# The pooling mixer multiplies by its weights first and takes the running means as a band of coefficients on TensorE

## The chip, the cores and the metric

The kernel runs on one core of a Trainium2 chip. A run's time is the device time of one execution in microseconds (us); the time of a kernel is the median of its runs. One execution is also profiled, and all rows below come from that one.

## What is computed

Two layers of a decoder on 512 tokens of 1024 channels. Each layer is a feed-forward network (FFN), a token mixer and a second FFN, each behind a norm with a learned shift and scale. The mixer of layer 0 is the pooling mixer, cut here to what matters:

```python
POOL_WINDOWS = (2, 4, 8, 16)      # one for each group of 256 channels
for gi, w in enumerate(POOL_WINDOWS):
    ...
    outs.append((cs[..., sl] - prev) / cnt - hf[..., sl])   # trailing mean of w tokens minus the token
pooled = jnp.stack(outs, axis=2)
mixed = jnp.einsum('bsgc,gcd->bsgd', pooled, w_grp.astype(jnp.float32))
return (mixed.reshape(b_, s_, d_) * scale.astype(jnp.float32)).astype(h.dtype)
```

The mean runs over tokens and the weights over channels, so the two can be taken in either order.

## The kernel before

Activations lie with channels on the 128 partitions: `x` is 128 x 8 x 512 (partition, channel tile `kt` or `dt`, token). The tokens are worked in two halves of 256 wherever a norm follows, so that one half is normed on the other engines while TensorE works on the other half.

An FFN ends in `closing`: for each half, eight output tiles `dt` of 18 matmuls each (three matmuls of 256 columns, `mm3`, for each of six weight tiles), so 144 matmuls a half. VectorE adds each result into `x` (`update`, L225), ScalarE squares it (L174), GpSimd adds the squares (L175). After a half, `pool_then` is called: `rsig` sums the squares over partitions with two one-column matmuls (L197), VectorE and GpSimd make the reciprocal root (L199, L201), VectorE lays it on a diagonal (L203), and one matmul spreads it over the partitions (L207).

Then `Pooling.means` norms the eight tiles of the half (VectorE `t` L387, ScalarE `h` L389), adds shifted copies until the window is full (L396, on GpSimd for the widest window, on VectorE for the others), repairs the first tokens (L401) and makes mean minus token (L412, tiles `made`). `mix` multiplies by the weights: two matmuls of 256 columns for each output tile (L422), `update`, and the sum of squares for the next norm on TensorE (`sumsq_pe`, L181, one matmul for each tile). `pool_then` for half 0 makes means only; for half 1 it mixes half 0, makes the means of half 1, norms half 0 for the next FFN (`norm`, L216 to L219), mixes half 1 and norms it. The next FFN begins with the same two halves, three weight tiles of 48 matmuls each (`up`).

Result tiles of TensorE come from a pool of five PSUM banks (`bank()`, tag `mm`), handed out in the order in which the program asks. Weights arrive by DMA as `raw`; ScalarE and VectorE split them into `wh` and `wl` (L151, L152). A scheduler puts the instructions of each engine into one fixed order when the kernel is built; an engine then takes them in that order.

Of the kernel before, what the change touches and what calls it, by code (L numbers as in the profile page):

```python
# [7 lines left out]
F32 = mybir.dt.float32  # L8
F32R = mybir.dt.float32r
AF = mybir.ActivationFunctionType  # L10
ALU = mybir.AluOpType
# [4 lines left out]
P = 128  # L16
D = 1024
KT = D // P
S = 512
# [9 lines left out]
GH = HEADS // NG  # L29
GC = GH * HD  # L30
WINDOWS = (2, 4, 8, 16)
EPS = 1e-6
BIG = 1e30
LAG = 3
# [2 lines left out]
HALVES = ((0, S // 2), (S // 2, S // 2))  # L37
# [3 lines left out]
def trunk(  # L41
    ctx: ExitStack,
    tc: tile.TileContext,
    x_in, x_rows, c_in, ada_w, ada_b, norm_g, w_in, w_out, w_end, pool_w, pool_scale,
    fox_qkv, fox_f, fox_bf, fox_gain, fox_o, consts, edges, out,
):
    nc = tc.nc
    pe, act, dve, gp = nc.tensor, nc.scalar, nc.vector, nc.gpsimd
# [7 lines left out]
    tmp = ctx.enter_context(tc.tile_pool(name="tmp", bufs=2))  # L56
# [8 lines left out]
    def bank(tag="mm"):  # L65
        return banks[tag].tile([P, S], F32, tag=tag, name=tag)
# [12 lines left out]
    ng = pers.tile([P, DEPTH * 3, KT], F32, name="ng")  # L79
    ab = pers.tile([P, DEPTH * 3, 3 * KT], F32, name="ab")  # L80
    x = pers.tile([P, KT, S], F32, name="x")
# [101 lines left out]
    def rsig(acc, t0, tn, summed=False):  # L183
# [10 lines left out]
        else:  # L194
            st = bank("s")
            for b in range(bn):
                pe.matmul(st[:, b:b + 1], acc[:, (b0 + b) * P:(b0 + b + 1) * P], ones[:, 0:1],  # L197
                          start=True, stop=True)
        dve.tensor_scalar(out=v[:, :bn], in0=st[:, :bn], scalar1=1.0 / D, scalar2=EPS,  # L199
                          op0=ALU.mult, op1=ALU.add)  # L200
# [21 lines left out]
    def update(y, i, dt, t0, tn, acc, gate=None, sums=sumsq):  # L222
        sl = slice(t0, t0 + tn)
        g = (mods[i]["g"] if gate is None else gate)[:, dt:dt + 1]
        dve.scalar_tensor_tensor(out=x[:, dt, sl], in0=y, scalar=g, in1=x[:, dt, sl],  # L225
                                 op0=ALU.mult, op1=ALU.add)
        if acc is not None:
            sums(acc, dt, t0, tn)
        else:
            nc.sync.dma_start(out[:, dt, sl], x[:, dt, sl])  # L230
# [5 lines left out]
    class Feed:  # L236


        def __init__(self, w):
            self.units = [(w_in[w, j], [P, 2, KT, P], 2) for j in range(JC)]  # L240
            for ci in range(2):
                self.units += [(w_out[w, ci, dt], [P, JC, P], 4) for dt in range(KT)]
                j0, nj = CHUNKS[ci + 1]
                self.units += [(w_in[w, j], [P, 2, KT, P], 2) for j in range(j0, j0 + nj)]
            self.units += [(w_end[w, u], [P, 16, P], 4) for u in range(KT * (NJ - 2 * JC) // 16)]
            self.made = []
            self.depth = len(slots["pools"])
# [113 lines left out]


    class Pooling:
        def __init__(self, i, pool, w):
            self.i, self.pool, self.w = i, pool, w
            self.scale = pool.tile([P, KT], F32, name="sc")
            nc.sync.dma_start(self.scale, pool_scale)
            dve.tensor_tensor(out=self.scale, in0=self.scale, in1=mods[i]["g"], op=ALU.mult)
            self.edges = pool.tile([P, 4, 16], F32, name="ed")
            nc.sync.dma_start(self.edges, edges)  # L370
            self.tails = pool.tile([P, KT, 16], F32, name="tails")
            gp.memset(self.tails, 0.0)

        def means(self, r, t0, tn):

            m = mods[self.i]
            sl = slice(t0, t0 + tn)
            hs, wins, made = {}, {}, {}
            for gi in (3, 0, 1, 2):
                eng, w = gp if gi == 3 else dve, WINDOWS[gi]  # L380
                two = slice(2 * gi, 2 * gi + 2)
                h = hs[gi] = self.pool.tile([P, 2, 16 + tn], F32, tag="h", name="h", bufs=3)
                eng.tensor_copy(h[:, :, :16], self.tails[:, two])
                for k in range(2):
                    kt = 2 * gi + k
                    t1 = tmp.tile([P, tn], F32, tag="t1", name="t1")
                    dve.scalar_tensor_tensor(out=t1, in0=x[:, kt, sl], scalar=m["a"][:, kt:kt + 1],  # L387
                                             in1=r[:, :tn], op0=ALU.mult, op1=ALU.mult)
                    act.activation(h[:, k, 16:], t1, AF.Identity, bias=m["s"][:, kt:kt + 1])  # L389
                if t0 == 0:  # L390
                    act.activation(self.tails[:, two], h[:, :, tn:], AF.Copy)
                cur, step = h, 1
                while step < w:
                    nxt = self.pool.tile([P, 2, 16 + tn], F32, tag=f"win{gi // 3}", name="win", bufs=2)
                    a = 16 - (w - 2 * step)
                    eng.tensor_tensor(out=nxt[:, :, a:], in0=cur[:, :, a:],  # L396
                                      in1=cur[:, :, a - step:16 + tn - step], op=ALU.add)
                    cur, step = nxt, 2 * step
                win = wins[gi] = cur[:, :, 16:]
                if t0 == 0:  # L400
                    eng.tensor_tensor(  # L401
                        out=win[:, :, :w - 1], in0=win[:, :, :w - 1],
                        in1=self.edges[:, gi, :w - 1].unsqueeze(1).to_broadcast([P, 2, w - 1]),
                        op=ALU.mult)
                if gi < 3:
                    made[gi] = self.pooled(gi, win, hs[gi])
            made[3] = self.pooled(3, wins[3], hs[3])
            return made

        def pooled(self, gi, win, h):  # L410
            made = self.pool.tile([P, 2, S // 2], F32, tag="made", name="made", bufs=4)
            dve.scalar_tensor_tensor(out=made, in0=win, scalar=1.0 / WINDOWS[gi], in1=h[:, :, 16:],  # L412
                                     op0=ALU.mult, op1=ALU.subtract)
            return made

        def mix(self, made, t0, tn):

            sums = bank()
            for dt in range(KT):
                y = bank()  # L420
                for ct in range(2):
                    pe.matmul(y[:, :tn], self.w[:, 2 * dt + ct], made[dt // 2][:, ct], start=ct == 0,  # L422
                              stop=ct == 1)
                update(y[:, :tn], self.i, dt, t0, tn, sums, gate=self.scale, sums=sumsq_pe)
            return sums

# [22 lines left out]
    def fox(i, early_pool, first, second_half, then):  # L449
        acc2 = new_acc()  # L450
        with tc.tile_pool(name="fox", bufs=1, reuse_waits="tile") as fp:
# [46 lines left out]
            def projections(grp):  # L498
# [18 lines left out]
                def block(role, b):  # L517
# [6 lines left out]
                    if role == 2:  # L524
# [8 lines left out]
                                      op=ALU.add)  # L533
                    dve.tensor_scalar(out=v, in0=v, scalar1=1.0 / HD, scalar2=EPS, op0=ALU.mult,
                                      op1=ALU.add)
# [181 lines left out]
    with tc.tile_pool(name="more", bufs=1, side="right", reuse_waits="tile") as more:  # L717
# [3 lines left out]
        with tc.tile_pool(name="start", bufs=2, reuse_waits="tile") as sp, in_order, ExitStack() as early:  # L721
# [15 lines left out]
            act.activation(cond, cond, AF.Silu)  # L737
            dve.tensor_scalar(out=v, in0=v, scalar1=1.0 / D, scalar2=EPS, op0=ALU.mult, op1=ALU.add)
            gp.tensor_tensor(out=v, in0=v, in1=mhalf[:, :NTB], op=ALU.pow)
# [33 lines left out]
            for kt in range(KT):  # L773
                t1 = sp.tile([P, S], F32, tag="t1", name="t1")
                act.activation(t1, x[:, kt], AF.Identity, scale=mods[0]["a"][:, kt:kt + 1],
                               bias=mods[0]["s"][:, kt:kt + 1])
# [23 lines left out]
        ahead = []  # L800
# [10 lines left out]
        with tc.tile_pool(name="poolw", bufs=1, side="right", reuse_waits="tile") as pw:  # L811
            pw_all = pw.tile([P, 16, P], F32, name="poolw")
            pooling = []
            opened = ExitStack()

            def pool_then(acc, t0, tn):
                r = rsig(acc, t0, tn)
                if t0 == 0:
                    pool = opened.enter_context(tc.tile_pool(name="pool", bufs=1, reuse_waits="tile"))
                    pooling.append(Pooling(1, pool, pw_all))  # L820
                    pooling.append(pooling[0].means(r, t0, tn))
                    return
                sums = pooling[0].mix(pooling[1], *HALVES[0])
                made = pooling[0].means(r, t0, tn)
                norm(2, sums, *HALVES[0], True)
                sums = pooling[0].mix(made, t0, tn)
                ahead.append(Feed(1))
                ahead[0].fetch(len(slots["pools"]))
                norm(2, sums, t0, tn, True)
                opened.close()  # L830

            jobs = ada_jobs(0, False) + ada_jobs(1)
            jobs += [(lambda pool: nc.sync.dma_start(pw_all, pool_w), lambda _: None)] + ada_jobs(2)
            feed = Feed(0)
            feed.units = feed.units[4:]
            ffn(0, feed, jobs, pool_then, begin, started=4)
# [80 lines left out]
```

## Time and profile before

| | |
|---|---|
| median of 3 runs | 1829.47 us (1829.47, 1829.47, 1833.93) |
| the profiled execution | 1832.36 us |
| its span | 1830.6 us |
| TensorE busy | 98% of the span |
| VectorE, ScalarE, GpSimd busy | 54%, 34%, 6% |

The span is what the profile shows; 1.8 us lie around it. TensorE is nearly always busy, so what matters is where it is not. Busy ends of matmuls are modelled; how fast they follow each other is read from their starts.

### The profile page before, as it was taken

Reading aid. Unit: us, or ns where it says so; the run is one execution under the profiler, and the core shown is the slowest. Engines: PE = TensorE matmul, PEld = TensorE weight load, DVE = VectorE, ACT = ScalarE, POOL = GpSimd, SP = SyncE. Lnnn points to the kernel's source line nnn. Section 1 sums busy time; section 2 is a strip of 40 time slices with the busy share of each in tenths; the row PEclk is TensorE's granted clock in tenths of the full one; section 3 lists DMA queues with packets and bytes.
Section 4 is the critical chain, followed back from the end, with each engine's and each line's share of the span. In section 5 each row is a group of like instructions: output and inputs, shape, how many; then the busy total and the mean of one; then the engine's idle time right before and its main releaser. Section 6 shows DMA issues by size and latency. Waiting matters only on the chain.

```text
span 1830.6 us, 24017 instructions
## 1 busy us (share of the span) xinstructions
PE 1794.5 (98%) x9564; PEld 1543.5 (84%) x9564; DVE 989.8 (54%) x1963; ACT 624.8 (34%) x1258; POOL 107.6 (6%) x118
## 2 busy tenths in 40 slices
PE   6999999989999999999999999999999999999999
PEld 5888888879888888998888889989997888888887
DVE  7567466386466473363453634577677553432433
ACT  6323223244223232242232333455454342222231
POOL 0000000050000000110000001221110200000000
PEclk9999999999999999999999999999999899999999
DMA  9457466211366452231543431122212021321421
GB/s 367 188 204 269 181 231 229 93 70 64 121 252 245 174 218 99 70 138 70 202 159 144 174 131 69 48 76 72 80 59 87 12 105 58 126 99 63 138 92 69
DMA packets 45857, 244.73 MB, mean 134 GB/s; under 512 B 5409, under 2 KB 10017, under 8 KB 21937
## 3 DMA queue, kind: packets, MB, share of 16 engines
q1 hardware_dynamic: 45744, 243.20, 36.3%
q8 instruction: 75, 1.23, 0.3%
q14 instruction: 38, 0.30, 0.1%
HBM read 241.05 MB, written 2.13 MB: 133 GB/s over the span
## 4 chain that ended last, share of the span: by engine, by line
PE 95%; DVE 4%; ACT 1%; issue 0%; DMA 0%; POOL 0%; SPq 0%; ACTq 0%; DVEq 0%; POOLq 0%
PE mm L164 28%; PE mm L165 27%; PE mm L163 27%; PE s L163 3%; PE s L165 3%; PE s L164 3%; PE mm L592 2%; DVE wl L152 1%; PE mm L618 1%; PE mm L595 1%; DVE x L225 0%; DVE win L396 0%; DMA rows<-x_rows 0%; DVE t L387 0%; PE mm L422 0%
## 5 line engine op out<-in xcount | busy, mean ns | idle before, releaser
L164 PE MATMUL mm<-hlo,wh 128*128 128x512 f32 (+1 forms) x1512 | 560.4, 372 | 2.8 <-DVE hlo L786 2.8
L165 PE MATMUL mm<-hhi,wl 128*128 128x512 f32 (+1 forms) x1512 | 558.0, 371 | 0.5 <-DVE wl L152 0.5
L163 PE MATMUL mm<-hhi,wh 128*128 128x512 f32 (+1 forms) x1512 | 554.5, 372 | 1.6 <-ACT hhi L777 1.3
L151 ACT ACTIVATE wh<-raw 128x256 fp32r<-128x256 f32 (+2 forms) x528 | 311.6, 654 | 576.6 <-PE mm L164 322.7
L152 DVE TENSOR_TENSOR wl<-raw,wh 128x256 fp32r<-128x256 f32 (+2 forms) x528 | 359.8, 734 | 59.0 <-ACT wh L151 54.8
L164 PEld LDWEIGHTS mm<-hlo,wh 128*128 128x128 f32 x1512 | 284.5, 188 | 52.3 <-DVE hlo L786 3.3
L163 PEld LDWEIGHTS mm<-hhi,wh 128*128 128x128 f32 x1512 | 283.2, 189 | 52.2 <-ACT hhi L777 1.7
L165 PEld LDWEIGHTS mm<-hhi,wl 128*128 128x128 f32 x1512 | 284.4, 188 | 49.9 <-DVE wl L152 0.7
L290 DVE TENSOR_TENSOR sil<-sil,mm 128x512 f32<-128x512 f32 (+1 forms) x95 | 61.0, 642 | 460.1 <-PE mm L165 443.0
L164 PE MATMUL mm<-gl,wh 128*128 128x512 f32 (+1 forms) x848 | 299.0, 353 | 0.0
L165 PE MATMUL mm<-gh,wl 128*128 128x512 f32 (+1 forms) x848 | 298.3, 353 | 0.0
L163 PE MATMUL mm<-gh,wh 128*128 128x512 f32 (+1 forms) x848 | 297.7, 354 | 0.0
L165 PEld LDWEIGHTS mm<-gh,wl 128*128 128x128 f32 x848 | 160.3, 189 | 21.9
L164 PEld LDWEIGHTS mm<-gl,wh 128*128 128x128 f32 x848 | 160.3, 189 | 21.9
L163 PEld LDWEIGHTS mm<-gh,wh 128*128 128x128 f32 x848 | 159.7, 189 | 22.0
L100 DVE CUSTOM_DVE_ANT_0 ada<-ada,cond 128x1024 f32<-128x1024 f32 x144 | 170.2, 1219 | 0.7 <-DMA ada<-ada_w 0.6
L289 ACT ACTIVATE sil<-mm 128x512 f32<-128x512 f32 (+1 forms) x94 | 52.5, 559 | 237.6 <-PE mm L165 236.4
L337 DVE SCALAR_TENSOR_TENSOR x<-mm,mg,x 128x512 f32<-128x512 f32 x64 | 48.0, 749 | 99.2 <-PE mm L165 98.3
L175 POOL TENSOR_TENSOR acc<-acc,sq 128x256 f32<-128x256 f32 x56 | 49.8, 889 | 866.3 <-ACT sq L174 535.2
L163 PE MATMUL s<-wh,hhi 128*128 128x256 f32 x288 | 84.2, 292 | 3.5 <-DVE qk L551 3.5
L165 PE MATMUL s<-wh,hlo 128*128 128x256 f32 x288 | 82.8, 288 | 0.0
L164 PE MATMUL s<-wl,hhi 128*128 128x256 f32 x288 | 82.6, 287 | 0.0
(173 smaller groups left out, 1656.6 us busy)
## 6 DMA issues: line engine op xcount, KB each, us to landing
raw<-w_in SPq DMA_DIRECT2D x84, 1024.0 KB, 5.1
ada<-ada_w SPq DMA_DIRECT2D x72, 1024.0 KB, 5.0
raw<-w_out SPq DMA_DIRECT2D x64, 512.0 KB, 5.6
raw<-w_end SPq DMA_DIRECT2D x12, 1024.0 KB, 4.8
raw<-fox_qkv SPq DMA_DIRECT2D x12, 1024.0 KB, 4.8
raw<-w_in SPq DMA_DIRECT2D x16, 256.0 KB, 8.0
cb<-cum SPq DMA_DIRECT2D x16, 256.0 KB, 3.4
raw<-fox_o SPq DMA_DIRECT2D x4, 1024.0 KB, 4.8
```

The source lines that it names most:

```text
L100: dve.tensor_tensor_reduce(out=raw[:, r, :], in0=raw[:, r, :], in1=cond, scale=1.0, scalar=0.0, op0=ALU.mult, op1=ALU.add, accum_out=mods[ ...
L151: act.activation(hi[:, c:c + n], src[:, c:c + n], AF.Copy)
L152: dve.tensor_tensor(out=lo[:, c:c + n], in0=src[:, c:c + n], in1=hi[:, c:c + n].bitcast(F32), op=ALU.subtract)
L163: pe.matmul(o, lh, rh, start=start, stop=False)
L164: pe.matmul(o, lh, rl, start=False, stop=False)
L165: pe.matmul(o, ll, rh, start=False, stop=stop)
L175: gp.tensor_tensor(out=acc[:, sl], in0=acc[:, sl], in1=sq, op=ALU.add)
L289: act.activation(sil[:, :tn], gu[0][:, :tn], AF.Silu)
L290: dve.tensor_tensor(out=sil[:, :tn], in0=sil[:, :tn], in1=gu[1][:, :tn], op=ALU.mult)
L337: done = dve.scalar_tensor_tensor(out=x[:, dt, :], in0=y, scalar=mods[i]["g"][:, dt:dt + 1], in1=x[:, dt, :], op0=ALU.mult, op1=ALU.add)
L592: pe.matmul(s[hh][:, :n], self.q[m == 2][rows, self.pair, b * P:n], self.k[m == 1][rows, self.pair, :n], start=m == 0, stop=False)
L595: pe.matmul(s[hh][:, b * P:n], mr[:, 0, :], mr[:, 1, :], start=False, stop=True)
```

## The change

The order of the two linear steps is turned round. `spread` makes the normed `h` as before, without windows. `product` multiplies: `h` is now the stationary operand (128 channels by 128 tokens) and the weights are the moving one, so that the result `z` has tokens on partitions; a half is two blocks of 128 tokens, 16 matmuls of 256 columns, and ScalarE copies four banks of 512 columns out to `z`. `mix` takes the means with a constant matrix `bands` of 128 x 143 for each window (mean minus token): for each output tile and block one matmul of 128 columns (`own`, L412) and, for every block but the first, one of 15 columns for the tokens that look back into the block before (`carry`, L416). All window work on VectorE and GpSimd, the tails and the edge repair are gone.

```diff
-        def means(self, r, t0, tn):
...
+        def spread(self, r, t0, tn):
...
+            h = self.pool.tile([P, KT, tn], F32, tag="h", name="h", bufs=2)
+            for kt in range(KT):
+                t1 = tmp.tile([P, tn], F32, tag="t1", name="t1")
+                dve.scalar_tensor_tensor(out=t1, in0=x[:, kt, t0:t0 + tn], scalar=m["a"][:, kt:kt + 1],
+                                         in1=r[:, :tn], op0=ALU.mult, op1=ALU.mult)
+                act.activation(h[:, kt], t1, AF.Identity, bias=m["s"][:, kt:kt + 1])
+            return h
+
+        def product(self, h, t0, tn):
+
+            ng = len(WINDOWS) // 2
+            for b in range(tn // P):
+                z = self.z[t0 // P + b] = self.pool.tile([P, D], F32, tag="z", name="z", bufs=3)
+                for c in range(2):
+                    o = bank()
+                    for g in range(ng):
+                        og = o[:, g * 2 * P:(g + 1) * 2 * P].rearrange("p (d q) -> p d q", q=P)
+                        for ct in range(2):
+                            gi = c * ng + g
+                            pe.matmul(og, h[:, 2 * gi + ct, b * P:(b + 1) * P], self.w[:, gi, ct],
+                                      start=ct == 0, stop=ct == 1)
+                    act.activation(z[:, c * S:(c + 1) * S], o, AF.Copy)
+
+        def mix(self, t0, tn):
 
             sums = bank()
             for dt in range(KT):
                 y = bank()
-                for ct in range(2):
-                    pe.matmul(y[:, :tn], self.w[:, 2 * dt + ct], made[dt // 2][:, ct], start=ct == 0,
-                              stop=ct == 1)
+                cols = slice(dt * P, (dt + 1) * P)
+                for b in range(tn // P):
+                    n = t0 // P + b
+                    own = self.bands[:, int(n == 0), dt // 2]
+                    pe.matmul(y[:, b * P:(b + 1) * P], self.z[n][:, cols], own[:, :P], start=True,
+                              stop=n == 0)
+                    if n:
+                        last = self.bands[:, int(n == 1), dt // 2]
+                        pe.matmul(y[:, b * P:b * P + REACH], self.z[n - 1][:, cols], last[:, P:],
+                                  start=False, stop=True)
                 update(y[:, :tn], self.i, dt, t0, tn, sums, gate=self.scale, sums=sumsq_pe)
             return sums
...
-                    pooling.append(pooling[0].means(r, t0, tn))
+                    pooling[0].product(pooling[0].spread(r, t0, tn), t0, tn)
                     return
-                sums = pooling[0].mix(pooling[1], *HALVES[0])
-                made = pooling[0].means(r, t0, tn)
+                sums = pooling[0].mix(*HALVES[0])
+                h = pooling[0].spread(r, t0, tn)
                 norm(2, sums, *HALVES[0], True)
-                sums = pooling[0].mix(made, t0, tn)
+                pooling[0].product(h, t0, tn)
+                sums = pooling[0].mix(t0, tn)
```

Line numbers shift by one in the changed kernel (L163 to L165 are L164 to L166, L197 is L198, L207 is L208), and the product stands in L399. The matmuls of the pooling mixer change as follows.

| | before | after |
|---|---|---|
| weights, 256 columns | 32 | 32 |
| `own`, 128 columns | 0 | 32 |
| `carry`, 15 columns | 0 | 24 |

**The first place, on TensorE's queue.** This is where half 0 of the closing of the first FFN has ended and its norm begins. Before, 37 matmuls of half 1 already stand ahead of the two one-column matmuls, and 32 and then 75 more follow with the spreading matmul between them:

```order
L165 MATMUL mm<-gh,wl 128x256
L163 MATMUL mm<-gh,wh 128x256
L197 MATMUL s<-ones,acc 128x1 x2
L164 MATMUL mm<-gl,wh 128x256
L165 MATMUL mm<-gh,wl 128x256
L163 MATMUL mm<-gh,wh 128x256
```

Now the 144th matmul of half 0 is the last one ahead of them:

```order
L164 MATMUL mm<-gh,wh 128x256
L165 MATMUL mm<-gl,wh 128x256
L166 MATMUL mm<-gh,wl 128x256
L198 MATMUL s<-ones,acc 128x1 x2
L208 MATMUL s<-dg,ones 128x256
L399 MATMUL mm<-poolw,h 128x256 x10
L164 MATMUL mm<-gh,wh 128x256
L165 MATMUL mm<-gl,wh 128x256
L166 MATMUL mm<-gh,wl 128x256
L164 MATMUL mm<-gh,wh 128x256
L399 MATMUL mm<-poolw,h 128x256 x6
```

What moved: the norm of half 0 and the whole product of half 0 (16 matmuls) now stand ahead of 140 of the 144 matmuls of half 1.

**The second place, on TensorE's queue.** This is the end of half 1 of the closing. Before, the weights follow (`made` by `poolw`), with a sum of squares (L181) among them:

```order
L165 MATMUL mm<-gh,wl 128x256
L422 MATMUL mm<-made,poolw 128x256 x2
L181 MATMUL mm<-sq,ones 128x256
L422 MATMUL mm<-made,poolw 128x256 x2
L197 MATMUL s<-ones,acc 128x1 x2
L422 MATMUL mm<-made,poolw 128x256 x4
```

Now:

```order
L166 MATMUL mm<-gh,wl 128x256
L412 MATMUL mm<-bands,z 128x128 x2
L416 MATMUL mm<-bands,z 128x15
L182 MATMUL mm<-sq,ones 128x256
L412 MATMUL mm<-bands,z 128x128 x2
L416 MATMUL mm<-bands,z 128x15
```

What moved: the sum of squares of the first output tile now stands behind three short matmuls.

**The third place, on ScalarE's queue**, at the same point of the program: the splitting of the third weight tile of the next FFN (`wh<-raw`) and the squares of the last closing tile (L175) and of the first mixed tiles (L181):

```order
L175 ACTIVATE sq<-x 128x256 x2
L152 ACTIVATE wh<-raw 128x1024
L175 ACTIVATE sq<-x 128x256
L152 ACTIVATE wh<-raw 128x1024
L175 ACTIVATE sq<-x 128x256 x2
L152 ACTIVATE wh<-raw 128x1024 x2
L175 ACTIVATE sq<-x 128x256
L181 ACTIVATE sq<-x 128x256 x5
```

Before, it stood like this:

```order
L389 ACTIVATE h<-t_2759,ms_919 128x256
L389 ACTIVATE h<-t_2762,ms_919 128x256
L174 ACTIVATE sq<-x 128x256
L391 ACTIVATE tails<-h 128x32
L151 ACTIVATE wh<-raw 128x1024 x2
L389 ACTIVATE h<-t_2775,ms_919 128x256
L174 ACTIVATE sq<-x 128x256
```

What moved: behind the third pair of splittings there stood an `h` and a square of half 1; now the last square of half 1 and all squares of the mix stand there.

## Rows read from the trace of the kernel before

**Rows 1.** Stretches of 10 us: PE, PEld, DVE, ACT, POOL busy; PEclk, DMA share, GB/s

```profile
380.00:390.00 10.00, 7.85 (x63) 7.39 (x61) 9.98 (x14) 7.54 (x16) 9.55 (x8) 1.00 0.30 105
390.00:400.00 10.00, 6.80 (x19) 5.53 (x20) 9.57 (x19) 2.01 (x6) 3.53 (x4) 0.66 0.56 206
400.00:410.00 10.00, 8.41 (x37) 6.43 (x35) 10.00 (x23) 6.01 (x14) 5.15 (x4) 1.00 0.00 0
```

**Rows 2.** Chain that ended last, from 360 to 440 us: start, us, what

```profile
373.30 0.34 PE s L197 x4
...
376.21 2.35 DVE wl L152 x2
...
381.33 0.98 DVE win L396
...
414.76 3.45 PE mm L422 x16
...
420.71 0.47 PE mm L163 x4
```

**Rows 3.** Tile `win` alone in one stretch: DVE busy, POOL busy, PEclk, DMA share, GB/s

```profile
374.00:426.00 52.00, 16.83 (x23) 10.80 (x9) 0.93 0.18 61
```

**Rows 4.** Timeline where half 0 ends: start, us, instruction, [idle before <-what ended it]

```profile
368.58 0.28 PE L165 MATMUL mm<-gh,wl 128*128 128x256 f32 x1
...
368.90 0.48 DVE L225 SCALAR_TENSOR_TENSOR x<-mm,mg,x 128x256 f32<-128x256 f32 x1 [1.68 <-PE mm L165]
...
370.04 0.74 POOL L175 TENSOR_TENSOR acc<-acc,sq 128x256 f32<-128x256 f32 x1 [1.42 <-ACT sq L174]
...
373.02 0.53 PEld L197 LDWEIGHTS s<-ones,acc 128*128 128x128 f32 x4
...
373.47 0.19 PEld L164 LDWEIGHTS mm<-gl,wh 128*128 128x128 f32 x1
...
373.68 0.16 DVE L199 TENSOR_SCALAR v<-s 128x2 f32<-128x2 f32 x1
...
373.91 0.71 POOL L201 TENSOR_TENSOR v<-v,mhalf 128x2 f32<-128x2 f32 x1 [3.13 <-DVE v L199]
```

**Rows 5.** Timeline of PE in the attention: six fp32 records of 128 columns

```profile
1408.75 0.84 PE L618 MATMUL mm<-ident,p 128*128 128x128 f32 x6
```

**Rows 6.** Timeline of DVE later: the diagonal, and the first normed tiles after a spread

```profile
398.84 0.42 DVE L203 TENSOR_TENSOR dg<-ident,v 128x256 f32<-128x256 f32 x1 [0.40 <-POOL v L201]
...
419.12 0.87 DVE L216 SCALAR_TENSOR_TENSOR t<-x,ma,s 128x256 f32<-128x256 f32 x2 [0.38 <-PE s L207]
```

**Rows 7.** Timeline of ACT: the third weight split, and one normed tile

```profile
386.90 2.00 ACT L151 ACTIVATE wh<-raw 128x1024 fp32r<-128x1024 f32 x2 [2.10 <-PE mm L164]
...
403.81 0.51 ACT L389 ACTIVATE h<-t,ms 128x256 f32<-128x256 f32 x1 [0.28 <-DVE t L387]
```

**Rows 8.** Groups of ACT by form: copy of a bank of 512 columns

```profile
L761 ACT ACTIVATE x<-s 128x512 f32<-128x512 f32 x8 | 4.6, 582 | 0.9 <-PE s L760 0.9
```

**Rows 9.** Stretches of 1 us in the pooling stage, columns as in rows 1

```profile
391.00:392.00 1.00, 0.00 (x0) 0.00 (x0) 1.00 (x4) 0.65 (x3) 0.00 (x0) 1.00 1.01 426
...
393.00:394.00 1.00, 1.00 (x4) 0.79 (x3) 1.00 (x1) 0.00 (x0) 0.53 (x1) 0.50 0.02 8
...
399.00:400.00 1.00, 1.00 (x5) 0.80 (x4) 1.00 (x3) 0.00 (x0) 0.00 (x0) 0.63 0.30 123
```

**Rows 10.** Stretches of 2 us at a wait of PE in the attention, columns as in rows 1

```profile
1204.00:1206.00 2.00, 0.65 (x6) 0.41 (x4) 2.00 (x7) 1.98 (x5) 0.00 (x0) 1.00 0.00 0
1206.00:1208.00 2.00, 0.58 (x5) 0.62 (x6) 1.83 (x6) 1.99 (x7) 0.00 (x0) 1.00 0.24 33
...
1210.00:1212.00 2.00, 2.00 (x11) 2.00 (x11) 0.42 (x1) 0.07 (x1) 0.00 (x0) 0.50 0.58 238
```

**Rows 11.** Stretches of 10 us at the end of the attention, columns as in rows 1

```profile
1410.00:1420.00 10.00, 8.33 (x36) 6.97 (x36) 7.02 (x27) 4.56 (x14) 0.00 (x0) 0.67 0.38 133
...
1430.00:1440.00 10.00, 9.69 (x50) 8.13 (x49) 5.59 (x14) 4.64 (x11) 0.00 (x0) 0.63 0.00 0
```

More of the change, by code (lines that the diff above doesn't have):

```diff
@@ L31 @@
 WINDOWS = (2, 4, 8, 16)
+REACH = max(WINDOWS) - 1
 EPS = 1e-6
@@ L44, in trunk @@
     x_in, x_rows, c_in, ada_w, ada_b, norm_g, w_in, w_out, w_end, pool_w, pool_scale,
-    fox_qkv, fox_f, fox_bf, fox_gain, fox_o, consts, edges, out,
+    fox_qkv, fox_f, fox_bf, fox_gain, fox_o, consts, bands, out,
 ):
@@ L364, in __init__ @@
         def __init__(self, i, pool, w):
-            self.i, self.pool, self.w = i, pool, w
+            self.i, self.pool = i, pool
+            self.w = w.rearrange("p (g d c) q -> p g c d q", d=2, c=2)
             self.scale = pool.tile([P, KT], F32, name="sc")
@@ L368, in __init__ @@
             dve.tensor_tensor(out=self.scale, in0=self.scale, in1=mods[i]["g"], op=ALU.mult)
[L369 to L372, printed above, removed]
-        def means(self, r, t0, tn):
-            m = mods[self.i]
[L377 to L416, printed above, removed]
+            self.bands = pool.tile([P, 2, len(WINDOWS), P + REACH], F32, name="bands")
+            nc.sync.dma_start(self.bands, bands)
@@ new lines, in __init__ @@
+            self.z = {}
+        def spread(self, r, t0, tn):
+            m = mods[self.i]
+            h = self.pool.tile([P, KT, tn], F32, tag="h", name="h", bufs=2)
[5 more added lines that the diff above has]
+            return h
@@ L881 @@
     consts = np.stack([np.eye(P), np.where(q[:, None] >= q[None, :], 0.0, BIG)], axis=1)
-    edge = np.ones((4, 16))
-    for gi, w in enumerate(WINDOWS):
-        edge[gi, :w - 1] = w / np.arange(1, w)
+    ahead = np.arange(P + REACH)[None, :] - q[:, None]
+    seen = np.arange(1, P + REACH + 1)[None, :]
+    band = [[np.where((ahead >= 0) & (ahead < w), 1.0 / (np.minimum(seen, w) if at_start else w), 0.0)
+             - (ahead == 0) for w in WINDOWS] for at_start in (False, True)]
     arrays = {
@@ L903 @@
         "consts": consts.astype(np.float32),
-        "edges": np.broadcast_to(edge.astype(np.float32), (P, 4, 16)),
+        "bands": np.array(band, np.float32).transpose(2, 0, 1, 3),
     }
```

## The prediction

> **What bounds the kernel now.** I read the page first: TensorE is busy for 98% of the span, so a change shows in the time where TensorE waits or where it gets more work. Then the table of stretches around the pooling mixer [rows 1]: from 380 to 410 us TensorE is busy for 7.9, 6.8 and 8.4 us of each 10, and VectorE for all of it. The chain of waits says the same [rows 2]: it leaves TensorE at 376 us for VectorE, runs through weight splits and window sums, comes back to TensorE for the weights at 414.8 us, and the next FFN's matmuls begin at 420.7 us. So here, and only for these some 40 us, VectorE is the bound, and the change takes work from it. The window work, `made` included, is 16.8 us on VectorE and 10.8 us on GpSimd [rows 3]. That is what the change removes. But VectorE's time is worth only what TensorE idles for, so I make the sum on TensorE.
>
> **TensorE before.** Half 0 of the closing ends with the matmul at 368.58 us [rows 4]; matmuls of 256 columns follow each other every 0.12 us (four in 0.47 us, [rows 2]), so TensorE is free of it at 368.7. From there to 420.7 are 52.0 us. The work in them, counted on its queue: 144 matmuls of half 1, 17.3; 32 matmuls with the pool weights at 0.43 (16 records of half a matmul in 3.45 us, [rows 2]), 13.8; 14 sums of squares of the same form, 6.0; 3 spreading matmuls, 1.3; 4 one-column matmuls, 0.9 (four loads from 373.02 to 373.47, [rows 4], so 0.22 each). Sum 39.3. TensorE thus has 12.7 us of idle time and of half clock to give. This is the most that the change can win; what it adds is set against it.
>
> **Added work.** The product is the 32 old matmuls in another order: 0. The band is 32 matmuls of 128 and 24 of 15 columns. An fp32 matmul is two records. Six fp32 records of 128 columns take 0.84 us with the last one's tail [rows 5], 0.11 each, so 0.22 for `own`. No row has 15 columns. Below it lies the matmul of one column at 0.22, where loading sets the pace, above it 0.43 for 256 columns; I take 0.22, as its two loads are the same. So 56 x 0.22 = 12.3 us. Bounds: 11 (if the records of `carry` follow at 0.085, as the chain's four in 0.34 us, [rows 2]) to 15 (at 0.13, the 0.53 us of the four loads whole).
>
> The Trainium skill, page "TensorE: Matmul & The Clock Gate", section "Back-to-back issue gap", would have it cheaper: it puts a matmul of up to 64 columns at some 60 cycles against 134 for 128 columns. By it a `carry` would be an estimated 0.05 us and the band some 8 us. The one-column row [rows 4] speaks against it, and the sum goes by the row.
>
> **First wait.** Before, the norm of half 0 costs TensorE nothing: 37, 32 and 75 matmuls of half 1 stand around its two stops. Now its one-column matmuls stand right behind the 144th matmul, and the product ahead of 140 matmuls of half 1, so nothing covers the norm. From 368.7: the last tile's update begins at 368.90, its square is added by 370.78 [rows 4], so TensorE idles 2.2 us. The two matmuls take 0.45; VectorE's `v` comes 0.66 after the first load (373.02 to 373.68), GpSimd's root 0.23 later for 0.71 [rows 4], the diagonal 0.42 [rows 6]: the spread starts at about 373.0, idle 1.6. It takes 0.43; a normed tile needs half of 0.87 on VectorE [rows 6] and 0.51 on ScalarE [rows 7], so the first product starts at 374.6, idle 1.2. Its eight tiles come every 0.5 us, with two buffers for `t`, against 0.43 of work: idle 0.5. Together 5.5 us, with 4.5 to 6.5 as bounds. The four copies to `z`, 0.58 each [rows 8], lie behind the other eight products and the 140 matmuls; without that cover they would cost 0.6.
>
> **The clock.** In the pooling stage the granted clock was at half from 393 to late in 399 to 400, after TensorE had stood still (391 to 392 is one row of that gap) [rows 9]. In the attention it also fell after 1204 to 1208, where TensorE worked for 1.2 of 4 us; by 1210 to 1212 it was 0.50 [rows 10]. The new first wait is 5.0 us of idle time with 0.9 of work in it, much like the second. So I expect half clock (1.2 GHz) for the first products: 0.86 instead of the 0.5 at which tiles come, 4 to 8 products, 1.4 to 2.9 us. I take 2; bounds 0 (no fall) and 5 (half of a stretch of 10 us, as in [rows 11]).
>
> The Trainium skill warns of this on the same page, section "HAM oscillation — how this bites in real kernels": groups of matmuls with waits between them are throttled anew after each wait. The trace agrees for the two waits named. [...]
>
> **Second wait.** Behind the end of half 1 on ScalarE now stand the two splits of the third weight tile, which wait for that end (before, too: 386.90, 2.00 us, idle until a matmul, [rows 7]), and only behind them the last square of half 1 and the first of the mix. Before, half 0's mix was waiting for VectorE anyway. Now TensorE's first sum of squares stands behind three short matmuls (0.66 us) and waits for 2.0 + two squares of at most 0.51 [rows 7]: 2.3 us idle. Bounds 0.5 and 3. VectorE has the same splits (1.1 us each, half of 2.35, [rows 2]) ahead of the next updates, which ends at the same time.
>
> **Third wait.** For half 1 the norm's stops lie among mixing and sums of squares; the last `z` copy, 0.58 [rows 8], is nearly covered by the spread behind it. I take 0.5; bounds 0 and 2.
>
> **Sum.** Up to the next FFN's first matmul the work is 39.3 + 12.3 - 1.3, as only 11 of the 16 sums of squares now stand ahead of it instead of 14, = 50.3. Idle 5.5 + 2 + 2.3 + 0.5 = 10.3. It starts at 368.7 + 60.6 = 429.3 instead of 420.7, and the three sums come back behind it: 8.6 + 1.3 = 9.9 us later. The norm of half 1 then lies under 144 matmuls of half 0, as before, and TensorE is busy without a gap behind, so nothing catches up. Against the profiled execution: 1832.4 + 9.9 = 1842.3 us. The median lies 2.9 below that execution: 1829.5 + 9.9 = 1839.4, and I say 1839. From the lower bounds of the work and the waits it would be 11 + 5.5 - 12.7 + 1.3 = +5, from the upper ones +19; they won't all meet, so the forecast's own range is +6 to +14 (1835 to 1843). What the measurement can tell from no change is about 0.3%, 5.5 us.
>
> **Rivals.**
> - *Narrow matmuls by their columns, or no fall of the clock: no difference.* If `carry` costs 15/256 of 0.43, the band is 7.6 instead of 12.3: +5.2, 1834.7; with the clock kept up, +7.9 alone, +3.2 with both. For it: the page's rule on few columns. Against: the one-column row and both falls. 15%.
> - *The clock stays down: worse.* Attention loses whole stretches at 0.63 to 0.67 granted clock [rows 11] though TensorE is 83 to 97% busy there. If the first wait starts such a stretch and the second another, at 5 us each, the term of 2 becomes 10: +18, 1847. 12%. [...]
> - *Faster: TensorE's idle time swallows the band.* VectorE is the bound of the stage by [rows 1, 2], and loses 16.8 us [rows 3]. If half 1's matmuls did cover the norm of half 0, the chain would be shorter by the window work on it, about 10 of the 16.8 us, 1819. For that the first wait must be under 1 us and the band under some 6 us, 0.1 for each matmul; it decides whether those 140 matmuls stand ahead of the product. They stand behind it, and with no wait at all my sum still has 12.3 + 1.3 - 12.7 = +0.9. 6%, mostly for gains elsewhere: the order in the attention moves too, where a stretch at full clock would give back up to 5 us [rows 11].
> - *The forecast*: 67%.
>
> **Numbers.** 1839 us. Slower by over 0.3%: the forecast and the worse case, 0.79. Within it 0.15, faster 0.06. For 8 in 10 the range runs from 1832, inside the no-difference case, to 1846, which leaves the worst of the second rival out.
>
> **What would show it.** Right: in the changed trace TensorE has an idle gap of 2 us ended by GpSimd's `acc`, one of 1.6 ended by the diagonal and one of 1.2 ended by `h`; a clock of 0.50 soon after; the closing's half 1 ending near 401 us instead of 386.8; `own` and `carry` both spaced at 0.22; one wait for `sq` behind the third `wh`; the next FFN at about 429. VectorE busy for well under 10 us in 10 from 380 on. Wrong: matmuls of half 1 in the first gap, `carry` at 0.05, or the difference arising behind 440 us.

## The result and the profile after

| | before | after |
|---|---|---|
| median of the runs | 1831.6 us (1829.5 to 1833.9, 4 runs) | 1848.0 us (1847.2 to 1848.9, 4 runs) |
| ratio, 95% interval | | 1.009 [1.0072, 1.0107] |
| the profiled execution, its span | 1832.4, 1830.6 us | 1847.7, 1845.9 us |

The change makes the kernel slower, by 16 us, 2 us beyond the upper end of the predicted range. Three marks that both traces share tell where the span's 15.3 us arose. "Pooling part" is from the first matmul of the closing to the spreading matmul of the second norm of the following FFN, "attention" is from the last spreading matmul ahead of it to the first one behind it.

| | before | after | difference |
|---|---|---|---|
| start to the first closing matmul | 351.4 | 351.9 | +0.5 |
| pooling part | 424.7 | 436.8 | +12.2 |
| attention | 297.8 | 300.6 | +2.7 |

From 788 to 1174 us of the new trace every mark stands 12.66 us later than before, so nothing arises in between. The +0.5 at the start is no more than executions differ by: over all kernels run here the first closing matmul starts at 351.4 to 351.9 us.

On the page of the kernel after, busy time of each engine:

```profile
PE 1809.8 (98%) x9676; PEld 1558.3 (84%) x9676; DVE 973.1 (53%) x1934; ACT 629.8 (34%) x1262; POOL 93.3 (5%) x106
```

TensorE's share is what it was. The stage shows in the stretches of 10 us of the kernel after (PE, PEld, DVE, ACT, POOL busy; PEclk, DMA share, GB/s), which answer to [rows 1]:

```profile
370.00:380.00 10.00, 6.07 (x16) 4.36 (x17) 4.10 (x10) 4.62 (x10) 1.43 (x2) 0.68 0.01 2
380.00:390.00 10.00, 10.00 (x65) 9.35 (x64) 0.97 (x2) 2.21 (x4) 0.00 (x0) 0.98 0.00 0
390.00:400.00 10.00, 10.00 (x86) 10.00 (x85) 5.97 (x8) 5.88 (x9) 4.68 (x5) 1.00 0.32 107
400.00:410.00 10.00, 7.99 (x67) 7.76 (x66) 6.70 (x13) 4.28 (x8) 4.20 (x4) 1.00 0.62 211
410.00:420.00 10.00, 9.97 (x52) 8.64 (x51) 5.86 (x17) 5.82 (x14) 0.70 (x1) 1.00 0.01 2
420.00:430.00 10.00, 8.41 (x65) 7.99 (x64) 7.34 (x19) 5.25 (x12) 0.00 (x0) 1.00 0.00 0
```

VectorE, full before, is now at 1.0 to 7.3 of 10 us. It was the bound of this stage, and taking 16.8 us from it gave nothing, because TensorE now has the band to do and holes of its own: in 370 to 380 (with a clock of 0.68), 400 to 410 and 420 to 430. The timeline of TensorE where half 0 ends, which answers to [rows 4], shows the first:

```profile
369.08 0.28 PE L166 MATMUL mm<-gh,wl 128*128 128x256 f32 x1
371.31 0.61 PE L198 MATMUL s<-ones,acc 128*128 128x1 f32 x4 [1.95 <-POOL acc L176]
373.42 1.05 PE L208 MATMUL s<-dg,ones 128*128 128x256 f32 x2 [1.50 <-DVE dg L204]
375.58 6.97 PE L399 MATMUL mm<-poolw,h 128*128 128x256 f32 x20 [1.11 <-ACT h L385]
382.21 0.47 PE L164 MATMUL mm<-gh,wh 128*128 128x256 f32 x1
```

These are the three gaps that were forecast, ended by `acc`, `dg` and `h`; no matmul of half 1 stands in them. In stretches of 1 us (the same columns as above) the clock falls at the second gap:

```profile
373.00:374.00 1.00, 0.58 (x2) 0.33 (x2) 0.36 (x1) 0.00 (x0) 0.00 (x0) 0.81 0.00 0
374.00:375.00 1.00, 0.47 (x2) 0.00 (x0) 0.49 (x2) 0.00 (x0) 0.00 (x0) 0.50 0.00 0
...
379.00:380.00 1.00, 1.00 (x3) 0.73 (x3) 0.00 (x0) 0.70 (x2) 0.00 (x0) 0.50 0.00 0
380.00:381.00 1.00, 1.00 (x5) 0.84 (x4) 0.00 (x0) 0.00 (x0) 0.00 (x0) 0.77 0.00 0
381.00:382.00 1.00, 1.00 (x7) 0.87 (x6) 0.00 (x0) 0.00 (x0) 0.00 (x0) 1.00 0.00 0
```

So the spread and most of the first ten products ran at 1.2 GHz. The timeline where half 1 ends shows the second hole:

```profile
402.13 0.28 PE L166 MATMUL mm<-gh,wl 128*128 128x256 f32 x1
...
402.33 2.00 ACT L152 ACTIVATE wh<-raw 128x1024 fp32r<-128x1024 f32 x2 [0.85 <-PE mm L165]
...
404.24 0.40 ACT L175 ACTIVATE sq<-x 128x256 f32<-128x256 f32 x1
404.55 0.40 ACT L181 ACTIVATE sq<-x 128x256 f32<-128x256 f32 x1
...
405.00 0.70 PE L182 MATMUL mm<-sq,ones 128*128 128x256 f32 x2 [2.01 <-ACT sq L181]
```

ScalarE takes the two splits of the third weight tile first, then the last square of the closing and the first of the mix, and TensorE waits 2.01 us. The chain of the kernel after (start, us, what) shows the third hole, and then the band:

```profile
421.94 0.45 PE s L208 x2
422.48 0.49 DVE t L217
422.99 0.80 ACT hhi L219 x2
423.84 0.43 ACT sq L181
424.31 0.70 PE mm L182 x2
...
425.36 0.32 PE mm L412 x2
425.67 0.13 PE mm L416 x2
425.80 0.32 PE mm L412 x2
...
432.03 0.21 PE mm L164
```

Behind the spread for the next FFN's half 0, VectorE and ScalarE take the first two normed tiles of that norm ahead of the first update and square of half 1's mix, and TensorE waits 1.59 us for that square:

```profile
424.31 0.70 PE L182 MATMUL mm<-sq,ones 128*128 128x256 f32 x2 [1.59 <-ACT sq L181]
```

In half 1 an `own` and its `carry` come every 0.445 us (425.36 to 425.80). The next FFN starts at 432.03, against 420.71 in [rows 2].

### The profile page after: what moved, and what is told of

Its sections match the earlier page's. It is cut to its first block, busy times and chain, and to the rows that moved or that the text cites. A ratio compares the mean times of both kernels' runs of the same rounds, so it can differ in the third digit from the quotient of the medians.

```text
span 1845.9 us, 24209 instructions
## 1 busy us (share of the span) xinstructions
PE 1809.8 (98%) x9676; PEld 1558.3 (84%) x9676; DVE 973.1 (53%) x1934; ACT 629.8 (34%) x1262; POOL 93.3 (5%) x106
## 4 chain that ended last, share of the span: by engine, by line
PE 96%; DVE 2%; ACT 1%; DMA 0%; issue 0%; POOL 0%; SPq 0%; DVEq 0%; ACTq 0%; POOLq 0%
PE mm L165 28%; PE mm L166 27%; PE mm L164 27%; PE s L164 3%; PE s L166 3%; PE s L165 3%; PE mm L586 2%; PE mm L612 1%; PE mm L399 1%; PE mm L589 1%; DVE wl L153 0%; PE mm L412 0%; PE mm L182 0%; DMA rows<-x_rows 0%; PE s L539 0%
## 5 line engine op out<-in xcount | busy, mean ns | idle before, releaser
L165 PE MATMUL mm<-hlo,wh 128*128 128x512 f32 (+1 forms) x1512 | 560.7, 372 | 2.6 <-DVE hlo L780 2.6
L166 PE MATMUL mm<-hhi,wl 128*128 128x512 f32 (+1 forms) x1512 | 559.1, 372 | 0.5 <-DVE wl L153 0.5
L164 PE MATMUL mm<-hhi,wh 128*128 128x512 f32 (+1 forms) x1512 | 556.7, 373 | 2.1 <-ACT hhi L771 1.8
L152 ACT ACTIVATE wh<-raw 128x256 fp32r<-128x256 f32 (+2 forms) x528 | 311.8, 654 | 564.5 <-PE mm L165 301.4
L165 PEld LDWEIGHTS mm<-hlo,wh 128*128 128x128 f32 x1512 | 284.5, 188 | 52.4 <-DVE hlo L780 3.2
L164 PEld LDWEIGHTS mm<-hhi,wh 128*128 128x128 f32 x1512 | 283.6, 189 | 52.4 <-ACT hhi L771 2.0
L166 PEld LDWEIGHTS mm<-hhi,wl 128*128 128x128 f32 x1512 | 284.6, 188 | 49.9 <-DVE wl L153 0.7
L165 PE MATMUL mm<-gl,wh 128*128 128x512 f32 (+1 forms) x848 | 299.3, 354 | 0.0
L166 PE MATMUL mm<-gh,wl 128*128 128x512 f32 (+1 forms) x848 | 298.4, 353 | 0.0
L164 PE MATMUL mm<-gh,wh 128*128 128x512 f32 (+1 forms) x848 | 297.9, 354 | 0.0
L165 PEld LDWEIGHTS mm<-gl,wh 128*128 128x128 f32 x848 | 160.4, 189 | 22.1
L166 PEld LDWEIGHTS mm<-gh,wl 128*128 128x128 f32 x848 | 160.4, 189 | 21.8
L164 PEld LDWEIGHTS mm<-gh,wh 128*128 128x128 f32 x848 | 159.7, 189 | 21.9
L164 PE MATMUL s<-wh,hhi 128*128 128x256 f32 x288 | 84.5, 293 | 3.2 <-DVE qk L545 3.2
L166 PE MATMUL s<-wh,hlo 128*128 128x256 f32 x288 | 82.8, 288 | 0.0
L165 PE MATMUL s<-wl,hhi 128*128 128x256 f32 x288 | 82.6, 287 | 0.0
```

The source lines that it names most:

```text
L152: act.activation(hi[:, c:c + n], src[:, c:c + n], AF.Copy)
L164: pe.matmul(o, lh, rh, start=start, stop=False)
L165: pe.matmul(o, lh, rl, start=False, stop=False)
L166: pe.matmul(o, ll, rh, start=False, stop=stop)
```

## The experiments

**The product asked for late.** The theory: the scheduler and the pools keep the program's order for result banks, so the product of half 0, written ahead of half 1's closing, holds back the 140 matmuls of half 1 while it waits for the norm. Here it is written behind them.

```diff
-                    pooling[0].product(pooling[0].spread(r, t0, tn), t0, tn)
+                    pooling.append(pooling[0].spread(r, t0, tn))
                     return
+                pooling[0].product(pooling[1], *HALVES[0])
                 sums = pooling[0].mix(*HALVES[0])
```

> The product of half 0 is called only after half 1 of the closing; all else is as in the changed kernel. Stage meant: from the last closing matmul of half 0 to the first matmul of the next FFN, 52.1 us before, 62.95 us in the changed kernel. Theory (the norm of half 0 stands uncovered because the product's banks are asked for ahead of half 1's): the first wait of 8.0 us and its half clock go, a wait of some 1 us for the last copies to z and 1 to 2 us for the norm of half 1 come: stage 55 to 57 us, clock 1.00 throughout, the run 5.5 to 8 us under the changed kernel's 1848. Rival (the band matmuls themselves are the price, and the wait only shifts where TensorE idles): stage 61 to 63 us, time as the changed kernel's.

Measured: 1834.3 us (10 runs), ratio to before 1.0009 [0.9999, 1.0019]; pooling part 426.7 us, 10.2 less than after and 2.0 more than before. The run is nearly 14 us under the changed kernel's 1848, where 5.5 to 8 were expected; 3.4 of them are a shorter attention (297.1 us). What TensorE waited for from 366 to 432 us in this kernel (total, times, longest), and one stretch of 10 us:

```profile
PE s L208 <- DVE dg L204: 1.1, 1, 1.1
PE mm L182 <- ACT sq L181: 0.5, 1, 0.5
```

```profile
370.00:380.00 10.00, 10.00 (x84) 9.95 (x84) 6.09 (x11) 4.06 (x9) 3.90 (x4) 1.00 0.04 7
```

The first hole is gone, the clock stays at 1.00, and the norm lies under half 1's matmuls. The second wait went too, since the product now stands between the end of the closing and the first square. Of the +2.0 that are left, 1.4 are the band of 12.5 less the 12.7 us of TensorE's old idle time and half clock, with the 1.6 us of waits that remain; the rest is less than two executions of the kernel before differ by (424.7 and 425.6, see below).

**Another pool for the product's banks.** The rest of the change is kept, but `product` takes its banks from the other pool (tag `s`), so that half 1's result tiles needn't queue behind it.

```diff
-                    o = bank()
+                    o = bank("s")
```

> Only the product's result tiles move: to the other PSUM pool (tag s, three banks) instead of the pool from which the closing's result tiles come. Theory (the order of handing out five banks holds half 1's 140 matmuls behind the product): they come ahead again, the product is spread among them, no wait of TensorE over 0.5 us before the end of the closing; the wait for the third weight split and first square (2.0 us) stays: stage 54 to 57 us, run 6 to 9 us under the changed kernel's 1848. Rival (the scheduler puts the product ahead by its own choice, or the added matmuls are the whole price): stage 61 to 63 us.

Measured: 1842.8 us (4 runs), ratio 1.0059 [1.0043, 1.0074]; pooling part 433.6, only 3.2 less than after, a miss. The timeline of TensorE in this kernel (three rows with waits) shows why:

```profile
396.83 0.70 PE L182 MATMUL mm<-sq,ones 128*128 128x256 f32 x2 [2.01 <-ACT sq L181]
409.74 0.93 PE L208 MATMUL s<-dg,ones 128*128 128x256 f32 x2 [2.73 <-DVE dg L204]
420.92 0.70 PE L182 MATMUL mm<-sq,ones 128*128 128x256 f32 x2 [1.08 <-ACT sq L181]
```

There is no wait around half 0's norm any more, but one of 2.73 us in its place: the spreading matmul of the next norm takes a bank of pool `s` too and is asked for ahead of half 1's product, which now waits behind it; the clock is at 0.83 in the stretch of 410 to 420 us that follows. That the trap had only moved to the other pool was tested with half 0's product alone in pool `s`:

```diff
-                    o = bank()
+                    o = bank("mm" if t0 else "s")
```

> As s_banks, but only half 0's product takes its banks from the other pool; half 1's takes them from the common one again. In s_banks the product of half 1 stood behind the spread of the next FFN's norm, which asks for a bank of the same pool first, and TensorE idled 5 us there with a fall of the clock. Theory (whoever asks for a bank first is waited for, in either pool): both traps are gone, what stays are the 2.0 us for the weight split and 1.6 us behind half 1's product; the part from the first closing matmul to the spread of the second norm of the next FFN, 424.7 us before, 436.8 changed, 433.6 in s_banks, becomes 429 to 430. Rival (the other pool is slow for this as such): 433 to 434.

Measured: pooling part 428.8 us, 8.0 less than after, and 1838.4 us in one run. TensorE's waits for `dg` and `acc` are gone from 366 to 432 us; two for `sq` stay:

```profile
PE mm L182 <- ACT sq L181: 3.6, 2, 2.0
```

So the order in which banks are asked for makes the first wait, in whichever pool, and the 8 us are its price with its half clock.

**Without the carry.** The 24 matmuls of 15 columns are left out, so the first tokens of a block miss their look back.

```diff
-                              stop=n == 0)
-                    if n:
+                              stop=True)
+                    if n > NTB:
```

> Leaves out the 24 matmuls of 15 columns, so tokens near a block's start lose the part of their mean from the block before. Theory (a narrow fp32 matmul costs its two loads, 0.22 us): the 24 are worth 5.3 us of stage, 62.95 to 57.7 us, with own at 0.22 us each. Rival (it costs by its columns, 0.05 us): 1.2 us, stage 61.7 us.

Measured: pooling part 431.7 us, 5.2 less than after: 0.215 us for each `carry` (5.16 / 24). TensorE's order in the attention moved too (296.3 us there), so the run's time of 1838.8 us says less. The one-column row of [rows 4] gave the right price, though these matmuls have 15 columns. The Trainium skill, page "TensorE: Matmul & The Clock Gate", section "Back-to-back issue gap", gives some 60 cycles for so narrow a matmul by itself; here, where each comes with its own stationary fp32 operand, it took 0.215 us.

**A warm first wait.** Four unread fp32 matmuls of 256 columns are added in the second gap of the first wait, where TensorE would stand still.

```diff
+            if warm:
+                w = bank("s")
+                for n in range(warm):
+                    pe.matmul(w[:, :tn], ones, acc[:, t0:t0 + tn], start=n == 0, stop=n == warm - 1)
...
-                r = rsig(acc, t0, tn)
+                r = rsig(acc, t0, tn, warm=0 if t0 else 4)
```

> Adds four fp32 matmuls of 256 columns, whose result nobody reads, into the first wait, between the one-column matmuls and the spread. Theory (TensorE's idle time there is what lets the clock fall): the granted clock stays at 1.00 or falls later, the ten first products take 0.43 to 0.5 us each instead of 0.70, stage 60 to 61 us, some 2.5 us less, though 1.7 us of work are added. Rival (the first products are paced by the normed tiles, the clock takes nothing): stage 62.95 us or 0.2 us more.

Measured: pooling part 434.6, 2.3 less than after; 1839.4 us in one run, of which 5.8 are a shorter attention (294.8 us). The stretch of 370 to 380 us has a clock of 1.00 in place of 0.68, and the first ten products take 4.6 us (375.00 to 379.62) where they took 6.6 (375.58 to 382.21), the waits for `acc` and `h` being the same (1.95 and 1.12 us):

```profile
371.48 1.97 PE L203 MATMUL s<-acc,ones 128*128 128x256 f32 x8
373.29 0.59 PE L212 MATMUL s<-dg,ones 128*128 128x256 f32 x2
375.00 4.97 PE L403 MATMUL mm<-poolw,h 128*128 128x256 f32 x20 [1.12 <-ACT h L389]
```

The clock's share of the first wait is thus 2.3 us, against 2 in the sum. (Two executions of the kernel after differ by 0.9 us in the pooling part, 436.8 and 437.7.)

**Half of the windows each way.** Windows 2 and 4 are summed on VectorE as before, 8 and 16 go by the band, and the product is asked for late. VectorE keeps some of the work that TensorE's matmuls hide, and the band halves. The core of the edit:

```diff
+                if dt < 4:
+                    for ct in range(2):
+                        pe.matmul(y[:, :tn], self.wall[:, 2 * dt + ct], made[dt // 2][:, ct],
+                                  start=ct == 0, stop=ct == 1)
+                else:
+                    cols = slice((dt - 4) * P, (dt - 3) * P)
```

> Windows 2 and 4 go the old way (shifted adds on VectorE, then weights), windows 8 and 16 the new one, with the product of half 0 called after the closing as in late_product. Theory (TensorE pays 0.22 us for each band matmul and has 12.7 us to give, if nothing waits): 28 band matmuls instead of 56, 6.2 us instead of 12.3; with 1.5 to 3 us of waits the same part takes 421.5 to 423.5 us, 1 to 3 us less than before, the run 0 to 4 us under the kernel before. Rival (VectorE, with 7 us of window work back, becomes the bound again): 425 us or more, as before or slower.

Measured: 1829.8 us (11 runs; before 1832.5, 15 runs), ratio 0.9988 [0.9979, 0.9997]; pooling part 422.3, where before took 424.7 and, in a second execution, 425.6. The interval just leaves out 1: a gain, though a small one, of 2.7 us. Its attention (296.4 us) lies within what before shows.

**Where the other 2.7 us come from.** All work in the attention is the same, but it took 2.7 us longer in the kernel after. First both kernels were profiled once more, unchanged.

> The kernel before, unchanged. The attention (between the two spreads at 1161.9 and 1459.8 us) took 297.8 us with 24 us of half clock in the profile of before, 300.6 and 31 in that of the changed kernel, 294.8 and 17 in warm. Theory (the order in the attention, which differs from build to build, sets it): 297.8 again within 0.5. Rival (where the clock's fall meets the same gaps differs from execution to execution): it differs by more than 1 us.

> The changed kernel, unchanged. Theory of the order: attention 300.6 us again within 0.5. Rival: it differs by more than 1 us, with the half clock. By both the pooling part takes 436.8 us within 1.

Measured: pooling part 425.6 us in before (424.7 the first time) and 437.7 in after (436.8); attention 295.8 us in before (297.8) and 300.5 in after (300.6). Half of that speaks for the order of instructions there, half against it. By the order that the scheduler wrote, TensorE's queue in the attention does differ between the two kernels, and a few unread matmuls in the second FFN are enough to change it. That allowed each kernel to be run with the other's order in the attention, and the kernel after with its own but 3.4 us later. The edit, with n = 4, 12 and 16:

```diff
+                    if i == 2 and j == j0 + ready and ci == 0:
+                        o = bank("s")
+                        for n in range(4):
+                            pe.matmul(o, wt[0][:, 0, 0], hhi[:, 0], start=n == 0, stop=n == 3)
```

> The kernel before with four unread matmuls of 512 columns (0.21 us each, 0.85 together) added in the second FFN; with them the scheduler gives TensorE in the attention exactly the order that the changed kernel has there. In the profiled executions so far the attention (first to next spreading matmul) took 297.8 and 295.8 us in the kernel before, 300.6 and 300.5 in the changed one, and longer where more of it ran at half clock. If the order in the attention causes this: about 300.5 us here, and the time 0.9 + 3.7 = 4.6 us over that of before. If it is where the attention's waits fall in time (its start moves by 0.9 us only): 295.5 to 298 us, and the time 0.9 us over that of before.

> The changed kernel with twelve such unread matmuls (2.6 us), with which TensorE's order in the attention is exactly that of the kernel before. If the order causes it: attention 295.5 to 298 us, and the time 1848 + 2.6 - 3.7 = about 1847 us. If it is the point in time: no forecast of the side, the attention anywhere in 295 to 301 us; 300.5 with the order of before would speak against the order, and the time would be 1850.6 us.

> The changed kernel with sixteen such unread matmuls (3.4 us); TensorE's order in the attention is that of the changed kernel. If the order causes its long attention: 300.5 us again, within 0.5. If it is the point in time, it may differ from that by 1 us and more.

Measured:

| kernel, order in the attention | attention | time |
|---|---|---|
| before, its own | 297.8, 295.8 | 1831.6 (4 runs), 1832.6 (13 runs beside the swaps) |
| after, that of before up to the last 27 us (swap_after) | 297.3 | 1846.9 (4 runs) |
| after, its own | 300.6, 300.5 | 1848.0 (4 runs) |
| after, its own, 3.4 us later (shift_after) | 300.6 | 1851.1 (1 run) |
| before, that of after (swap_before) | 301.4 | 1835.3 (10 runs) |

By the traces swap_before has the order of after throughout. swap_after has that of before only up to 1447 us; behind it the last products (`mm<-pt,v`) and the output projection (`mm<-ot,wh`, `mm<-ot,wl`) take turns in another way, 10, 12, 10 and 11 matmuls where before has 24 and 23, so this kernel is not the exact swap that was meant. With this said, the two orders don't overlap, in either kernel. swap_after came out within 0.2 us of the order's forecast. swap_before is 2.6 us over before beside it (ratio 1.0019 [1.0009, 1.0028]), between the two forecasts of 4.6 and 0.9; its profiled execution was the slowest of its ten (1838.1), so 301.4 is on the high side. The place is one stretch of 20 us near the attention's end (columns as above), of before, after, swap_after and swap_before:

```profile
1420.00:1440.00 20.00, 18.87 (x87) 15.40 (x86) 10.71 (x31) 8.15 (x23) 0.00 (x0) 0.65 0.00 1
```

```profile
1432.70:1452.70 20.00, 19.09 (x68) 14.49 (x68) 9.54 (x30) 7.40 (x22) 0.00 (x0) 0.51 0.00 0
```

```profile
1435.30:1455.30 20.00, 19.19 (x93) 16.20 (x93) 10.45 (x30) 7.69 (x22) 0.00 (x0) 0.67 0.00 1
```

```profile
1422.20:1442.20 20.00, 19.08 (x68) 14.62 (x66) 9.22 (x30) 7.17 (x21) 0.00 (x0) 0.50 0.00 1
```

TensorE is busy for 18.9 to 19.2 us in all four. With the order of before (in swap_after for the first 12 us of the stretch) the clock is at 0.65 and 0.67, with that of after at 0.51 and 0.50: 20 x 0.14 = 2.8 us of full-clock time less. The order isn't everything, though: the kernel with banks from the other pool and the one without the carry have the same order in the attention and took 299.6 and 296.3 us there. So the order is shown to move the attention by some 3 us; why the clock falls lower with the one than with the other is not shown.

## Why the prediction was right or wrong

The direction was right, and so was the mechanism in the pooling stage. What failed was one wait there, the attention, which the sum took as unchanged, and the point of reference. On TensorE from the end of half 0's closing (369.2) to the next FFN (432.0) there are now 62.8 us, against 60.6 in the sum. By its steps:

- *Band 12.3*: right. Eight tiles of half 0 (two `own`, one `carry`) at 0.67 us and sixteen blocks of half 1 (one of each) at 0.445 make 12.5, and no_carry confirms the price of the narrow ones. The first rival (a band of 7.6) is refuted.
- *First wait 5.5 and clock 2*: right in cause and nearly in size. From 369.2 to 382.2 are 13.0 us; the work in them is ten products at 0.43, a spread at 0.43 and the two one-column matmuls, 5.2, so 7.8 us are lost against 7.5. late_product and s_half0 show the cause, warm the clock's share of 2.3.
- *Closing of half 1*: 20.0 us from there to its end at 402.25 with 19.9 of work, +0.2. It ended 1.2 later than the 401 forecast.
- *Second wait 2.3*: right. 2.01 of idle time, and the matmul behind it takes 0.70 in place of 0.43.
- *Third wait 0.5*: too small, and this is the step of the stage that failed. It cost 1.59 + 0.27 = 1.9, near its upper bound of 2. The prediction looked for it at the last `z` copy, which is covered; it was the next norm's first tiles that stand ahead of the mix on VectorE and ScalarE.
- *Three sums of squares behind, +1.3*: right. The start of the next FFN, counted from the first closing matmul, moved by 10.8 us (80.1 after it, 432.03 less 351.93, instead of 69.3), the pooling part by 12.2.
- *"TensorE is busy without a gap behind, so nothing catches up"*: true up to 1174 us, where the shift is still 12.66. But the sum took the attention as unchanged, and that is the larger failure in the kernel: +2.7 us. The text had a moved order there only as a possible gain of up to 5 us, under the faster rival; it can cost as well. The prediction's own sign of being wrong, a difference behind 440 us, was seen.

The misses add up: 9.9 forecast, 2.2 in the stage, 2.7 in the attention and 0.5 at the start make the span's 15.3 us. That puts the profiled execution 5.4 us over the 1842.3 of the sum. The other 3.2 us of the miss are the step from there to the median: the prediction took 2.9 off, because the first three runs of before had their median that far under the profiled execution, and the median of after lies 0.3 over its own. The 2.9 were an accident of three runs: one more run raised the median of before to 1831.6, and beside the experiments it was 1832.5 to 1832.6 in 13 to 15 runs each, as in the profiled execution. Without the attention's 2.7 us the time would have been about 1845.3 us and within the range; with 1842.3 as the forecast the miss would have been 5.7 us.

The second rival (the clock stays down, +18) came near to the time, but not by its mechanism. It had a second stretch of half clock behind the second wait, and the clock is 1.00 in the rows of 400 to 410 and 420 to 430. The Trainium skill, page "TensorE: Matmul & The Clock Gate", section "HAM oscillation — how this bites in real kernels", tells of a kernel whose groups of matmuls are parted by long waits and throttled anew after each; the trace agrees for the first wait, of 4.6 us in three gaps, and shows no fall behind the second and third, of 2.01 and 1.59 us, which are shorter than that kernel's waits. The faster rival named its condition rightly: the 140 matmuls stood behind the product. late_product meets the condition and is still no gain (1.0009). The sum said so of a change without any wait, though its +0.9 is a slip: the 1.3 us of the three sums of squares leave the stage and come back behind it, so they cancel, and it is 12.3 - 12.7 = -0.4; with the 1.6 us of waits that late_product has left, +1.2, and its pooling part gave +2.0. By the same slip, and with 5.5 in place of 5.0 us of waits, the lower bounds were added up to +5 where they give 11 + 5.0 - 12.7 = +3.3. The forecast of 9.9 is not touched by either.

## What to carry to other kernels

When work moves to the busiest engine to relieve another, count first how much idle time that engine has in this stage: here 12.7 us, just what the band costs, so the best possible was a draw. A step that waits for a norm should be asked for behind the independent matmuls that are to cover it, because result banks are handed out in program order and everything asked for later from the same pool queues behind it; taking another pool only helps if nothing in that pool has the same problem. And where the scheduler rewrites the order far from the change, allow for a few us of either sign there.

## What was not expected of the hardware

The same matmuls of the attention took 294.8 to 301.4 us in thirteen profiled executions. In the four whose stretches are shown the difference lay in the granted clock, which over 20 us was 0.50 to 0.67 although TensorE was busy for 19 of them. In the pooling stage the clock fell behind gaps of 1.95 and 1.50 us with 0.6 us of work between them, and not behind a single gap of 2.01 us with a busy TensorE on both sides. An fp32 matmul of 15 columns cost 0.215 us, about as much as one of 128 (own and carry together come every 0.445); this the sum had expected, from the row with one column.
